# Bidirectional RWKV-7 scan in one kernel: state and v in one contraction, v transposed plainly and centred at the readout

## The chip, the cores and the metric

One core of one Trainium2 chip runs the whole layer in one launch. The metric is the device time in microseconds; less is better. Engines are called as the profile calls them: PE (matmuls, with PEld for its weight loads), DVE (vector), ACT (scalar), POOL and SP (which issues the DMAs).

## The reference, cut to what matters

A layer with two branches that share one input: a bidirectional RWKV-7 time mixing and a gated convolution. The sequence is 256 context and 2048 latent tokens, the width 1024, in 16 heads of 64. The change concerns the scan and its readout:

```python
def step(s, inp):                                  # s: heads x 64 x 64, for each direction
    rt, wt, kt, vt, at, bt = inp
    sa = jnp.einsum('bhij,bhj->bhi', s, at)
    s_new = s * wt[:, :, None, :] + sa[..., None] * bt[:, :, None, :] + vt[..., None] * kt[:, :, None, :]
    y = jnp.einsum('bhij,bhj->bhi', s_new if inclusive else s, rt)
    return s_new, y
...
mu = jnp.mean(y_sum, axis=-1, keepdims=True)       # the readout, per head of 64
var = jnp.mean(jnp.square(y_sum - mu), axis=-1, keepdims=True)
yn = ((y_sum - mu) * lax.rsqrt(var + LNX_EPS)).reshape(b, t, WIDTH_A) * lnx_w + lnx_b
```

## The kernel before, in words

**The first part** (to about 1650 us) projects the input, shifts and mixes it, and writes for each of 8 pairs of heads the factors of the scan to DRAM: `bkD` (b and k), `arD` (a and r), `vD` (v) and `TA`, `TB` (the inverse of the triangular system within a chunk), in fp32.

**The scan** goes over the pairs and, in each, over 36 chunks of 64 tokens; both directions `d` run side by side. Four chunks make a step `g`, of which there are 72. A generator, `prep(g + 1)`, makes the next step ready while `chunk` works on step `g`. Two heads share the 128 partitions, in halves of 64.

`prep` (L801) loads `bk` (one buffer, one DMA), `ar` (two halves, one a head, into a tile with zeros elsewhere, two buffers), `vvz` (one DMA) and six pieces of `Tt`. For each direction it transposes `bk` into `BK` (L828, copied by ACT in L831); multiplies v with `cen`, the matrix that takes the mean over 64 off, which transposes v as well (L835), of which ACT copies the lower half into `UV` (L838); multiplies `bk` with `ar` into the scores (L843), and masks them on DVE into `sc` (L847).

`chunk` (L882) has a chain that goes from one chunk to the next. x is the product of `ar` with the state `Sc` (L887) plus that of the scores `sc` with `UV` (L888), for each direction. Its two diagonal blocks of 64 are copied to `xs`, one by DVE (L890), one by ACT (L891). The product of `Tt` and `xs` (L895) gives u, which ACT puts into the upper half of `UV` (L896). POOL scales the old state (L902), the product of `BK` and `UV` (L909) gives its increment, and one DVE instruction a direction on 128x128 (L910) writes the new state. Beside the chain stand the outputs y (L917, L918), collected by ACT (L931) or DVE (L933).

`readout` (L853) comes twice a pair, for two segments of 512 tokens each time: a square on ACT (L857), a product that sums it over a head (L859), logarithm and exponential on ACT (L860, L863), then scale, gate and store.

**What sets the order.** `tick` (L1243) is called nine times a chunk. It hands out a share of the filling work: the dense fp16 matmuls of the gates and of the convolution's input (L360, with weights split on ACT and DVE in L200 and L201), the 31 taps of the convolution on DVE (L946), and later the projections of the convolution branch (L1106); and every third time a piece of `prep`. The instruction streams of each engine are then ordered by a scheduler when the kernel is built, so what stands behind what on an engine is read from the built order; each engine works off its stream in order.

**After the scan** (from about 3810 us) come the last projections and the output rows.

## Time and profile before

| | |
|---|---|
| three runs | 4125.75, 4129.82, 4140.15 us; median 4129.82 |
| the profiled execution | 4134.31 us, of which the profile's span is 4132.6 us |
| granted TensorE clock, mean | 0.978 of full |
| busy share of the span | PE 93%, PEld 58%, DVE 71%, ACT 47%, POOL 12% |
| chain that ended last, by engine | PE 49%, DVE 29%, ACT 10%, DMA 7%, issue 5% |
| DMA | 528.73 MB, mean 128 GB/s; 298116 of 520450 packets under 512 B |

One execution is profiled. The page first gives shares of the whole span, which mix stages with different limits; then 40 slices of it; then the chain of work that ended last and the costliest groups of instructions by line. A group's row has the count, the busy time, the mean duration, and the idle time of the engine just before its instructions with what ended most of it. Durations of matmuls overlap, so their rate is read from starts in the timeline.

### The profile page before, as it was taken

The numbers are of one execution on the slowest core, as the hardware profiler recorded it, in microseconds if no ns is written. First come the engines' busy times: TensorE is split into PE (matmuls) and PEld (weight loads), VectorE is DVE, ScalarE is ACT, GpSimd is POOL, SyncE is SP. The second block draws the span as 40 slices with busy tenths as digits, with TensorE's granted clock in tenths as the row PEclk, the third lists the DMA queues.
The fourth block names the chain that finished last, engine by engine and source line by source line (L and its number), as shares of the span: only waits on it lengthen the run. The fifth ranks groups of instructions, "written<-read, shape, count | busy, mean of one in ns | idle before, by whom it ended". The sixth has DMA issues, their size and how long they took to land.

```text
span 4132.6 us, 79379 instructions
## 1 busy us (share of the span) xinstructions
PE 3862.6 (93%) x30672; PEld 2396.1 (58%) x30672; DVE 2941.0 (71%) x6826; ACT 1941.7 (47%) x3594; POOL 490.1 (12%) x931
## 2 busy tenths in 40 slices
PE   8999999999999997999999999999999899899999
PEld 3444444444444443777776777777676566786444
DVE  5578788688788777698897998994445774334644
ACT  5666665666666554233324343333444452334522
POOL 0000000000000000231321222221111011110000
PEclk9999999999999998999999999999999999999999
DMA  5344443444444333435334244344535543534632
GB/s 204 126 166 144 158 162 133 138 151 166 141 166 140 139 137 110 92 77 136 70 81 131 71 112 98 85 123 129 142 96 162 161 139 107 156 75 113 203 101 76
DMA packets 520450, 528.73 MB, mean 128 GB/s; under 512 B 298116, under 2 KB 363012, under 8 KB 519560
## 3 DMA queue, kind: packets, MB, share of 16 engines
q1 hardware_dynamic: 520072, 523.66, 42.0%
q8 instruction: 241, 3.95, 0.4%
q14 instruction: 137, 1.12, 0.1%
HBM read 298.01 MB, written 196.35 MB: 120 GB/s over the span
## 4 chain that ended last, share of the span: by engine, by line
PE 49%; DVE 29%; ACT 10%; DMA 7%; issue 5%; SPq 1%; POOL 0%; DVEq 0%; ACTq 0%
PE pg L360 10%; PE pp L1106 5%; DVE acc L946 5%; DVE X L476 3%; DVE tmp L475 3%; PE psc L843 3%; PE px L895 3%; PE psy L909 3%; PE pvt L835 2%; PE px L887 2%; PE py L918 2%; PE py L917 2%; PE px L888 2%; DVE sc L847 1%; DMA wf<-in_w_in_dram 1%
## 5 line engine op out<-in xcount | busy, mean ns | idle before, releaser
L946 DVE SCALAR_TENSOR_TENSOR acc<-z,cw,acc 128x512 f32<-128x512 f32 x960 | 687.3, 750 | 10.9 <-ACT acc L944 3.7
L360 PE MATMUL pg<-hH,whi 128*128 128x512 f16 x1536 | 589.1, 384 | 7.8 <-ACT whi L200 7.0
L360 PE MATMUL pg<-hH,wlo 128*128 128x512 f16 x1536 | 587.5, 383 | 1.8 <-DVE wlo L201 1.8
L360 PE MATMUL pg<-hL,whi 128*128 128x512 f16 x1536 | 588.6, 383 | 0.0
L902 POOL TENSOR_SCALAR pre<-Sc,PL 128x128 f32<-128x128 f32 x560 | 357.6, 648 | 1577.2 <-DVE Sc L910 1438.1
L360 PEld LDWEIGHTS <-whi 128*128 128x128 f16 x3072 | 298.9, 99 | 261.0 <-issue 35.1
L891 ACT ACTIVATE xs<-px 64x128 f32<-64x128 f32 x288 | 78.3, 272 | 552.2 <-DVE xs L890 537.7
L209 PE MATMUL pg<-hH,whi 128*128 128x512 f16 x832 | 318.8, 384 | 4.2 <-ACT hH L279 4.0
L210 PE MATMUL pg<-hL,whi 128*128 128x512 f16 x832 | 319.6, 384 | 0.1
L211 PE MATMUL pg<-hH,wlo 128*128 128x512 f16 x832 | 319.3, 384 | 0.0
L910 DVE SCALAR_TENSOR_TENSOR Sc<-psy,PL,pre 128x128 f32<-128x128 f32 x560 | 173.0, 344 | 195.3 <-PE psy L909 191.5
L847 DVE TENSOR_TENSOR sc<-psc,msk 128x512 f32<-128x512 f32 (+1 forms) x288 | 180.1, 654 | 98.5 <-PE psc L843 97.5
L887 PE MATMUL px<-Sc,arz 128*128 128x128 f32 x1152 | 235.5, 286 | 7.1 <-DVE Sc L910 3.6
L895 PE MATMUL px<-xs,Tt 128*128 128x128 f32 x1152 | 193.8, 291 | 49.1 <-ACT xs L891 46.2
L360 PEld LDWEIGHTS <-wlo 128*128 128x128 f16 x1536 | 152.2, 99 | 134.3 <-issue 17.3
L888 PE MATMUL px<-UV,sc 128*128 128x128 f32 x1152 | 224.2, 276 | 0.0
L895 PEld LDWEIGHTS px<-xs,Tt 128*128 128x128 f32 x1152 | 155.2, 191 | 114.3 <-ACT xs L891 100.8
L843 PE MATMUL psc<-arz,bk 64*128 64x128 f32 (+1 forms) x2304 | 216.4, 290 | 4.7 <-ACT BK L831 2.2
L909 PE MATMUL psy<-UV,BK 128*128 128x128 f32 x1120 | 191.6, 294 | 24.7 <-ACT UV L896 24.6
L843 PEld LDWEIGHTS psc<-arz,bk 64*128 64x128 f32 x2304 | 176.0, 189 | 62.7 <-issue 39.5
L917 PE MATMUL py<-arz,Sc 128*128 128x128 f32 x1024 | 201.2, 278 | 1.8 <-DVE y L933 1.1
L887 PEld LDWEIGHTS px<-Sc,arz 128*128 128x128 f32 x1152 | 180.9, 192 | 34.7 <-DVE Sc L910 11.5
(361 smaller groups left out, 8137.2 us busy)
## 6 DMA issues: line engine op xcount, KB each, us to landing
wf<-in_w_in_dram SPq DMA_DIRECT2D x74, 512.0 KB, 3.7
bk<-bkD SPq DMA_DIRECT2D x72, 512.0 KB, 3.8
arz<-arD SPq DMA_DIRECT2D x144, 256.0 KB, 4.8
bkD<-bk SPq DMA_DIRECT2D x64, 512.0 KB, 2.7
arD<-ar SPq DMA_DIRECT2D x64, 512.0 KB, 3.6
vvz<-vD SPq DMA_DIRECT2D x72, 256.0 KB, 3.2
lt<-loD SPq DMA_DIRECT2D x32, 512.0 KB, 4.8
sh<-raw SPq DMA_DIRECT2D x64, 191.6 KB, 2.4
```

What stands on the lines that cost most here:

```text
L209: PE.matmul(ps, whi[:, k, :], xhi(k), start=(k == 0), stop=False)
L210: PE.matmul(ps, whi[:, k, :], xlo(k), start=False, stop=False)
L211: PE.matmul(ps, wlo[:, k, :], xhi(k), start=False, stop=(k == NK - 1))
L360: PE.matmul(ps, wt[a][:, k, :], b[:, k, o:o + 512], start=(m == 0), stop=(m == 23))
L843: PE.matmul(ps[h][:, c, :nq], bk[h * 64:h * 64 + 64, d, c, :], ar[h * 64:h * 64 + 64, d, c, :nq // 64, h, :], start=True, stop=True)
L887: PE.matmul(px[:, d, :], ar[:, d, c, 0].rearrange("p h l -> p (h l)"), Sc[d][k % 2], start=True, stop=True)
L888: PE.matmul(px[:, d, :], sc[:, d, c, 0].rearrange("p h l -> p (h l)"), UV[:, d, c, :], start=False, stop=True, skip_group_check=True)
L895: PE.matmul(px[:, 2 + d, :], t[:, d, c, :], xs[:, d, :], start=True, stop=True)
L902: G.tensor_scalar(pr, Sc[d][k % 2], pl, 1.0, op0=ALU.mult, op1=ALU.mult)
L909: PE.matmul(psy, BK[:, d, c, :], UV[:, d, c, :], start=True, stop=True)
L917: PE.matmul(o, Sc[d][k % 2], ar[:, d, c, 1].rearrange("p h l -> p (h l)"), start=True, stop=True)
L946: V.scalar_tensor_tensor(acc, z[:, k + 512 * i:k + 512 * i + 512], cw[:, k:k + 1], acc, op0=ALU.mult, op1=ALU.add)
```

## The change

The state gets a tile of its own kind, `SV`, of 128x128 for each chunk and direction: on the diagonal the two states, off the diagonal v of the two heads. The masked scores of the first kind go from `sc` into the zero blocks of `ar`. So x is one product of 128 rows of contraction where there were two, and its blocks off the diagonal are left as they come. `Tt` becomes block diagonal, u is written on the diagonal of `UV` and v off it, `bk` has b and k in swapped order for the second head, and only diagonal blocks of the state's increment are used, so the state update becomes four pieces of 64x64. v is transposed with `ident`, not multiplied with `cen`; the mean is taken off y in the readout, by a product with `cen`. x is copied by one ACT instruction.

```diff
@@ prep
-        nc.sync.dma_start(bk, bkD[p][:, :, ks].rearrange("p d c i l -> p d c (i l)"))
-        ar, vv = ars[g % NAR], vvs[0]
+        nc.sync.dma_start(bk[0:64], bkD[p][0:64, :, ks].rearrange("p d c i l -> p d c (i l)"))
+        for i in range(2):
+            nc.sync.dma_start(bk[64:128, :, :, 64 * i:64 * i + 64], bkD[p][64:128, :, ks, 1 - i, :])
+        ar, SV, vv = ars[g % NAR], SVs[g % NAR], vvz
         for h, hs in enumerate(H2):
             nc.sync.dma_start(ar[hs, :, :, :, h, :], arD[p][hs, :, ks])
-        nc.sync.dma_start(vv[:, :, 64:], vD[p][:, :, 256 * s:256 * s + 256])
+            nc.sync.dma_start(vv[hs, :, 64 * (1 - h):64 * (1 - h) + 256], vD[p][hs, :, 256 * s:256 * s + 256])
...
-        G.memset(UV[0:64], 0.0)
...
-                PE.matmul(pv[:, c, :], vv[:, d, c * 64:c * 64 + P], cen, start=True, stop=True)
...
-            S.activation(UV[64:128, d], pv[64:128], AF.Copy)
+                PE.transpose(pv[:, c, :], vv[:, d, c * 64:c * 64 + P], ident)
+            for x in (SV, UV):
+                for h, hs in enumerate(H2):
+                    S.activation(x[H2[1 - h], d, :, hs], pv[H2[1 - h], :, hs], AF.Copy)
...
             for h in range(2):
-                V.tensor_tensor(sc[:, d, :, :ni, h, :], ps[h].rearrange("p c (i l) -> p c i l", l=64)[:, :, :ni], msk[:, d:d + 1, :nq].rearrange("p o (i l) -> p o i l", l=64).broadcast_to([P, 4, ni, 64]), op=ALU.mult)
+                ho = H2[1 - h]
+                V.tensor_tensor(ar[ho, d, :, 0, h, :], ps[h][ho, :, 0, :], msk[ho, d:d + 1, 0:64].broadcast_to([64, 4, 64]), op=ALU.mult)
+                if s > 0:
+                    V.tensor_tensor(sc[:, d, :, h, :], ps[h][:, :, 1, :], msk[:, d:d + 1, 64:128].broadcast_to([P, 4, 64]), op=ALU.mult)
@@ readout
         for i in ii:
+            pc = pC.tile([P, 512], F32, name="pc", tag="pC")
+            PE.matmul(pc, cen, ys[i], start=True, stop=True)
+            S.activation(ys[i], pc, AF.Copy)
@@ chunk
         for d in range(2):
-            PE.matmul(px[:, d, :], ar[:, d, c, 0].rearrange("p h l -> p (h l)"), Sc[d][k % 2], start=True, stop=True)
-            PE.matmul(px[:, d, :], sc[:, d, c, 0].rearrange("p h l -> p (h l)"), UV[:, d, c, :], start=False, stop=True, skip_group_check=True)
-        xs = xss[k % 2]
-        V.tensor_copy(xs[0:64, :, 0:64], px[0:64, 0:2, 0:64])
-        S.activation(xs[64:128, :, 64:128], px[64:128, 0:2, 64:128], AF.Copy)
+            PE.matmul(px[:, d, :], ar[:, d, c, 0].rearrange("p h l -> p (h l)"), SV[:, d, c, :], start=True, stop=True)
+        xs = bp.tile([P, 2, P], F32, name="xs")
+        S.activation(xs, px[:, 0:2, :], AF.Copy)
...
-        S.activation(UV[0:64, :, c, :], px[0:64, 2:4, :], AF.Copy)
+        for hs in H2:
+            S.activation(UV[hs, :, c, hs], px[hs, 2:4, hs], AF.Copy)
...
-                V.scalar_tensor_tensor(Sc[d][(k + 1) % 2], psy, PL[:, p, d, k + 1:k + 2], pre[d], op0=ALU.mult, op1=ALU.add)
+                for hs in H2:
+                    V.scalar_tensor_tensor(Sn[hs, d, (c + 1) % 4, hs], psy[hs, hs], PL[hs, p, d, k + 1:k + 2], pre[d][hs, hs], op0=ALU.mult, op1=ALU.add)
```

The scheduler orders the new streams anew. Three places in them follow. On PE, the piece of one chunk (the 153rd) from x on, before; `pg` is a dense matmul, its weight loads stand as rows of their own, and a v product and that for u follow:

```order
L887 MATMUL px<-Sc_18661,arz_18648 128x128
L888 MATMUL px<-UV,sc 128x128
L887 MATMUL px<-Sc_18663,arz_18648 128x128
L888 MATMUL px<-UV,sc 128x128
L360 LDWEIGHTS whi
L360 MATMUL pg<-hH,whi 128x512
L360 LDWEIGHTS whi
L360 MATMUL pg<-hL,whi 128x512
L360 LDWEIGHTS wlo
L360 MATMUL pg<-hH,wlo 128x512
L360 LDWEIGHTS whi
L360 MATMUL pg<-hH,whi 128x512
```

and such a piece of the changed kernel, from x to u (its lines have other numbers):

```order
L890 MATMUL px<-SV_18650,arz_18648 128x128 x2
L359 LDWEIGHTS whi
L359 MATMUL pg<-hH,whi 128x512
L359 LDWEIGHTS whi
L359 MATMUL pg<-hL,whi 128x512
L359 LDWEIGHTS wlo
L359 MATMUL pg<-hH,wlo 128x512
L359 LDWEIGHTS whi
L359 MATMUL pg<-hH,whi 128x512
L896 MATMUL px<-xs,Tt_18646 128x128 x2
```

Four products for x have become two; dense matmuls stand between x and u in both. On DVE, a piece of the scan with the convolution before (`acc` is a tap of the convolution):

```order
L847 TENSOR_TENSOR sc<-psc,msk 128x8x64 x2
L890 COPY xs_18652<-px 64x2x64
L946 SCALAR_TENSOR_TENSOR acc<-z,cw,acc 128x512 x3
L910 SCALAR_TENSOR_TENSOR Sc_18660<-psy,PL,pre 128x128
L910 SCALAR_TENSOR_TENSOR Sc_18662<-psy,PL,pre 128x128
L946 SCALAR_TENSOR_TENSOR acc<-z,cw,acc 128x512 x2
L890 COPY xs_18651<-px 64x2x64
```

and of the changed kernel:

```order
L950 SCALAR_TENSOR_TENSOR acc<-z,cw,acc 128x512 x3
L845 TENSOR_TENSOR arz_18649<-psc,msk 64x4x64
L847 TENSOR_TENSOR sc<-psc,msk 128x4x64
L845 TENSOR_TENSOR arz_18649<-psc,msk 64x4x64
L847 TENSOR_TENSOR sc<-psc,msk 128x4x64
L950 SCALAR_TENSOR_TENSOR acc<-z,cw,acc 128x512 x3
L914 SCALAR_TENSOR_TENSOR SV_18651<-psy,PL,pre 64x64 x4
```

The copy of x has left the stream; scores and state come in twice as many pieces, of half and a quarter of the size. On ACT, a readout before, from the copy of x to that of u (`f` and `whi` belong to the filling work):

```order
L891 ACTIVATE xs_18651<-px 64x2x64
L674 ACTIVATE f_23518<-pg,un 128x512
L860 ACT_TABLE_LOAD
L860 ACTIVATE sqy<-pv,eps 128x512 x2
L863 ACT_TABLE_LOAD
L863 ACTIVATE sqy<-sqy 128x512 x2
L200 ACTIVATE whi<-wf,p2s 128x1024
L874 ACTIVATE y<-y,par 128x512 x2
L896 ACTIVATE UV<-px 64x2x128
```

and one of the changed kernel:

```order
L858 ACTIVATE y<-pc 128x512
L860 ACTIVATE sqy<-y 128x512
L898 ACTIVATE UV<-px 64x2x64 x2
L863 ACT_TABLE_LOAD
L863 ACTIVATE sqy<-pv,eps 128x512
L858 ACTIVATE y<-pc 128x512
L866 ACT_TABLE_LOAD
L866 ACTIVATE sqy<-sqy 128x512
L860 ACTIVATE sqy<-y 128x512
L199 ACTIVATE whi<-wf,p2s 128x1024
L877 ACTIVATE y<-y,par 128x512
L863 ACT_TABLE_LOAD
```

The logarithms of the two segments no longer stand side by side, so a readout has four table loads where it had two. Over the whole order the loads at these two lines go from 18 and 18 to 32 and 31, and one more comes at a gate.

## Rows read from the trace of the kernel before

**Rows 1.** Busy tenths of PE and DVE in 40 slices of the span:

```profile
PE   8999999999999997999999999999999899899999
DVE  5578788688788777698897998994445774334644
```

**Rows 2.** Windows of the scan: busy us (count) of PE, PEld, DVE, ACT, POOL:

```profile
1669.00:1819.00 150.00, 145.17 (x1081) 116.33 (x1080) 118.28 (x239) 48.20 (x119) 41.25 (x54) 1.00 0.37 86
1819.00:2783.00 964.00, 925.63 (x6583) 695.22 (x6581) 877.11 (x1796) 353.15 (x726) 237.78 (x301) 1.00 0.39 99
2783.00:3137.00 354.00, 338.08 (x2423) 257.15 (x2422) 170.07 (x454) 144.55 (x297) 53.93 (x108) 1.00 0.47 124
3137.00:3509.00 372.00, 350.62 (x2204) 235.06 (x2203) 223.86 (x497) 159.60 (x327) 42.35 (x77) 0.98 0.50 143
3509.00:3807.00 298.00, 266.47 (x1886) 222.90 (x1885) 115.60 (x304) 103.95 (x230) 46.20 (x103) 0.96 0.46 118
```

**Rows 3.** The same for L887 alone (PE, PEld), four PE records a chunk:

```profile
1819.00:2783.00 964.00, 107.86 (x528) 83.12 (x528) 1.00 0.39 99
2783.00:3137.00 354.00, 38.69 (x192) 30.13 (x193) 1.00 0.47 124
3509.00:3807.00 298.00, 39.71 (x192) 30.54 (x192) 0.96 0.46 118
```

**Rows 4.** Timeline of PE in one chunk (start us, us, what):

```profile
2313.45 0.39 PE L888 MATMUL px<-UV,sc 128*128 128x128 f32 x2
2313.67 0.39 PE L887 MATMUL px<-Sc,arz 128*128 128x128 f32 x2
2313.89 0.39 PE L888 MATMUL px<-UV,sc 128*128 128x128 f32 x2
```

**Rows 5.** Groups on PE (count | busy us, mean ns | idle before, releasers):

```profile
L888 PE MATMUL px<-UV,sc 128*128 128x128 f32 x1152 | 224.2, 276 | 0.0
L835 PE MATMUL pvt<-cen,vvz 128*128 128x128 f32 x1152 | 161.2, 280 | 6.6 <-ACT sqy L860 6.6
L828 PE MATMUL pbk<-ident,bk 128*128 128x128 f32 x576 | 111.4, 279 | 5.3 <-DMA bk<-bkD 2.4 <-DVE sc L847 1.4 <-ACT sqy L860 1.0
```

**Rows 6.** Timeline of DVE in the convolution stretch:

```profile
2310.91 0.59 DVE L910 SCALAR_TENSOR_TENSOR Sc<-psy,PL,pre 128x128 f32<-128x128 f32 x2
2311.43 2.72 DVE L946 SCALAR_TENSOR_TENSOR acc<-z,cw,acc 128x512 f32<-128x512 f32 x4
2314.08 1.27 DVE L847 TENSOR_TENSOR sc<-psc,msk 128x512 f32<-128x512 f32 x2
2315.28 0.27 DVE L890 COPY xs<-px 64x128 f32<-64x128 f32 x1
2315.48 0.73 DVE L946 SCALAR_TENSOR_TENSOR acc<-z,cw,acc 128x512 f32<-128x512 f32 x1
```

**Rows 7.** Groups on DVE, the scores and a product of half their size:

```profile
L847 DVE TENSOR_TENSOR sc<-psc,msk 128x512 f32<-128x512 f32 x256 | 167.6, 683 | 91.1 <-PE psc L843 90.6
L583 DVE TENSOR_TENSOR Asb<-pA,mk 128x256 f32<-128x256 f32 x64 | 26.9, 420 | 48.3 <-PE pA L582 29.9 <-PE pf L497 12.5 <-DMA cu<-Asb 3.4
```

**Rows 8.** Groups on ACT, the copies of v, u and x:

```profile
L838 ACT ACTIVATE UV<-pvt 64x512 f32<-64x512 f32 x144 | 85.1, 591 | 99.2 <-PE pvt L835 98.1
L896 ACT ACTIVATE UV<-px 64x256 f32<-64x256 f32 x288 | 108.1, 375 | 154.0 <-PE px L895 151.2
L891 ACT ACTIVATE xs<-px 64x128 f32<-64x128 f32 x288 | 78.3, 272 | 552.2 <-DVE xs L890 537.7 <-DVE p2t L170 4.7 <-DVE p2s L174 3.3
```

**Rows 9.** Timeline of ACT at a readout, from the copy of x to that of u:

```profile
2900.55 0.27 ACT L891 ACTIVATE xs<-px 64x128 f32<-64x128 f32 x1
2900.84 1.28 ACT L860 ACT_TABLE_LOAD   x1
2902.14 1.26 ACT L860 ACTIVATE sqy<-pv,eps 128x512 f32<-128x512 f32 x2
...
2905.77 0.36 ACT L896 ACTIVATE UV<-px 64x256 f32<-64x256 f32 x1
```

**Rows 10.** DMA issues of the page's last part (count, KB each, us to landing):

```profile
bk<-bkD SPq DMA_DIRECT2D x72, 512.0 KB, 3.8
arz<-arD SPq DMA_DIRECT2D x144, 256.0 KB, 4.8
```

More of the change, by code (lines that the diff above doesn't have):

```diff
@@ L59 @@
 PB = (1,)
-PV = ()
 SWP = 1
@@ L789 @@
     ars = [b1.tile([P, 2, 4, 2, 2, 64], F32, name=f"arz{i}") for i in range(NAR)]
-    vvs = [b1.tile([P, 2, 64 + 256], F32, name=f"vvz{i}") for i in range(1)]
-    xss = [b1.tile([P, 2, P], F32, name=f"xs{i}") for i in range(2)]
-    for t in Tt + ars + xss:
+    SVs = [b1.tile([P, 2, 4, P], F32, name=f"SV{i}") for i in range(NAR)]
+    vvz = b1.tile([P, 2, 64 + 256], F32, name="vvz")
+    for t in Tt + ars:
         G.memset(t, 0.0)
-    for t in vvs:
-        G.memset(t[:, :, 0:64], 0.0)
-    Sc = [[b1.tile([P, P], F32, name=f"Sc{d}{i}") for i in range(2)] for d in range(2)]
+    G.memset(vvz[0:64, :, 0:64], 0.0)
+    G.memset(vvz[64:128, :, 256:320], 0.0)
     st = {}
@@ L816, in prep @@
             o = 64 * h
-            nc.sync.dma_start(t[o:o + 32, :, :, 0:32], ta5[0, :, h, :, ks, :])
-            nc.sync.dma_start(t[o + 32:o + 64, :, :, 32:64], ta5[1, :, h, :, ks, :])
-            nc.sync.dma_start(t[o:o + 32, :, :, 32:64], tb5[:, h, :, ks, :])
-        sc = bp.tile([P, 2, 4, 2, 2, 64], F32, name="sc")
+            nc.sync.dma_start(t[o:o + 32, :, :, o:o + 32], ta5[0, :, h, :, ks, :])
+            nc.sync.dma_start(t[o + 32:o + 64, :, :, o + 32:o + 64], ta5[1, :, h, :, ks, :])
+            nc.sync.dma_start(t[o:o + 32, :, :, o + 32:o + 64], tb5[:, h, :, ks, :])
+        sc = bp.tile([P, 2, 4, 2, 64], F32, name="sc")
         BK = bp.tile([P, 2, 4, P], F32, name="BK")
         UV = bp.tile([P, 2, 4, P], F32, name="UV")
-        G.memset(UV[0:64], 0.0)
         yield
@@ L834, in prep @@
             for c in range(4):
-                PE.matmul(pv[:, c, :], vv[:, d, c * 64:c * 64 + P], cen, start=True, stop=True)
-                if c in PV:
-                    yield
-            S.activation(UV[64:128, d], pv[64:128], AF.Copy)
+                PE.transpose(pv[:, c, :], vv[:, d, c * 64:c * 64 + P], ident)
+            for x in (SV, UV):
+                for h, hs in enumerate(H2):
+                    S.activation(x[H2[1 - h], d, :, hs], pv[H2[1 - h], :, hs], AF.Copy)
             yield
-            ps = [pC.tile([P, 4, P], F32, name="psc", tag="pC") for _ in range(2)]
+            ps = [pC.tile([P, 4, 2, 64], F32, name="psc", tag="pC") for _ in range(2)]
+            ni = 1 if s == 0 else 2
             for c in range(4):
-                for h in range(2):
-                    PE.matmul(ps[h][:, c, :nq], bk[h * 64:h * 64 + 64, d, c, :], ar[h * 64:h * 64 + 64, d, c, :nq // 64, h, :], start=True, stop=True)
-                if c in PY:
-                    yield
+                for h, hs in enumerate(H2):
+                    PE.matmul(ps[h][:, c, :ni, :], bk[hs, d, c, :], ar[hs, d, c, :ni, h, :], start=True, stop=True)
             for h in range(2):
-                V.tensor_tensor(sc[:, d, :, :ni, h, :], ps[h].rearrange("p c (i l) -> p c i l", l=64)[:, :, :ni], msk[:, d:d + 1, :nq].rearrange("p o (i l) -> p o i l", l=64).broadcast_to([P, 4, ni, 64]), op=ALU.mult)
+                ho = H2[1 - h]
+                V.tensor_tensor(ar[ho, d, :, 0, h, :], ps[h][ho, :, 0, :], msk[ho, d:d + 1, 0:64].broadcast_to([64, 4, 64]), op=ALU.mult)
+                if s > 0:
+                    V.tensor_tensor(sc[:, d, :, h, :], ps[h][:, :, 1, :], msk[:, d:d + 1, 64:128].broadcast_to([P, 4, 64]), op=ALU.mult)
             yield
-        st[g] = dict(ar=ar, sc=sc, BK=BK, UV=UV)
+        st[g] = dict(ar=ar, sc=sc, BK=BK, UV=UV, SV=SV)
     ys = {}
@@ L901, in chunk @@
                 pl = PL[:, p, d, k + 1:k + 2]
-                G.tensor_scalar(pr, Sc[d][k % 2], pl, 1.0, op0=ALU.mult, op1=ALU.mult)
+                G.tensor_scalar(pr, SV[:, d, c, :], pl, 1.0, op0=ALU.mult, op1=ALU.mult)
                 pre.append(pr)
@@ L906, in chunk @@
         if k < NCH - 1:
+            Sn = SVs[(p * 9 + (k + 1) // 4) % NAR]
             for d in range(2):
@@ L916, in chunk @@
                 o = py[:, d, c % 2, :]
-                PE.matmul(o, Sc[d][k % 2], ar[:, d, c, 1].rearrange("p h l -> p (h l)"), start=True, stop=True)
-                PE.matmul(o, UV[:, d, c, :], sc[:, d, c, 1].rearrange("p h l -> p (h l)"), start=False, stop=True, skip_group_check=True)
+                PE.matmul(o, SV[:, d, c, :], ar[:, d, c, 1].rearrange("p h l -> p (h l)"), start=True, stop=True)
+                PE.matmul(o, UV[:, d, c, :], sc[:, d, c].rearrange("p h l -> p (h l)"), start=False, stop=True, skip_group_check=True)
                 if d == 0:
@@ L1262 @@
         if s == 0:
-            for d in range(2):
-                V.memset(Sc[d][0], 0.0)
+            for hs in H2:
+                V.memset(SVs[g % NAR][hs, :, 0, hs], 0.0)
         prv[0] = prep(g + 1) if g + 1 < NSTEP else None
```

4 lines of the change are left out of this document (1 added, 3 removed).

## The prediction

> **What bounds the kernel now.** I read the slices first, because they show where the scan begins: from the seventeenth slice on, PE stays at nine tenths, while DVE is near full only as long as the convolution runs, and then falls to four tenths [rows 1]. So I cut the scan into five stretches and asked for the busy time of each engine [rows 2]. They are: a start; the long stretch with the convolution (DVE busy 877 of 964 us); a stretch where the dense matmuls L360 still run but the convolution is over (DVE 170 of 354); one in which the projections of the convolution branch ride along; and a last one with nearly no filling work. The matmuls of L887 come four records to a chunk, so their counts give the pace [rows 3]: 528 records are 132 chunks at 964 / 132 = 7.30 us, 192 are 48 chunks at 354 / 48 = 7.38 us, and the last 48 chunks take 298 / 48 = 6.21 us. The reader is to see this: with the convolution and without it a chunk takes the same time, so DVE, although it is 91% busy in the first, does not set the pace. PE does, being 95 to 96% busy in both. In the last stretch PE falls to 89%, and the chain inside a chunk shows.
>
> **What goes from PE.** In a run of matmuls the starts lie 0.22 us apart for one fp32 product of two records [rows 4]: L888 at 2313.45, the next at 2313.67, the next at 2313.89. That is 0.11 us a record; the longer durations overlap. The change drops L888: 1152 records by 0.11 = 127 us [rows 5]. The v products of L835 have 1152 records for 576 products, whereas the transposes of L828 have 576 records for as many results [rows 5]; v is now a transpose, so 576 records go, 63 us. The readout adds 32 products of 512 columns, four times as wide as those at 0.22: 0.88 us each, 28 us. Net: 127 + 63 - 28 = **162 us less on PE**, or 162 / 288 = 0.56 us a chunk. The number of scores, of state and of y products is as before.
>
> **What DVE gains and loses.** The copy of x goes: 288 by 0.20 us (2315.28 to the next start at 2315.48 [rows 6]) = 58 us. The state update is cut in four: two pieces of 128x128 took 0.52 us to the next start (2310.91 to 2311.43 [rows 6]), 0.26 each. No row shows a 64x64 piece. From above it costs as much as the whole, 0.26; from below half, 0.13. The convolution steps, four times as long, start 0.66 us apart (2.65 us to 2314.08 for four [rows 6]), a slope of 0.40 us for 384 columns, so 64 columns fewer save 0.07: I take 0.19. Then 1120 by 0.19 less 560 by 0.26 = 213 - 146 = +67 us (bounds 0 and +146). The scores: 256 of 128x512 at 683 ns and 32 of the size of L583 at 420 ns [rows 7] make 188 us; after it 288 + 256 = 544 pieces of 256 columns at 420 ns make 228: +40. Net **+49 us**, 0.17 a chunk (bounds -18 to +128). What DVE also loses is a wait: before, the copy stood among the convolution steps and waited for PE, and ACT's half of x waited for it.
>
> **What ACT gets.** Four copies of 64x256 for one of 64x512: 576 by 375 ns less 144 by 591 = +131 us; x as one 128x256 piece, which I price as 64x256, 375 for 272 ns, 288 times: +30; u in two pieces of 64x128, 272 ns each, for one of 375: 288 by 169 ns = +49 [rows 8]. The readout adds 32 copies of 128x512, about 0.6 us as the 64x512 of L838: +19. The instruction order of the change has 63 table loads at the logarithm and the exponential where there were 36, and one more elsewhere: 28 by 1.28 us [rows 9] = +36. Together **+265 us** on an engine that is 353 / 964 = 37% busy in the convolution stretch [rows 2], so it will stand near half. Most of it runs beside PE's dense matmuls. The readout's part does not: there the copy of u, which the chain needs, stands behind both table loads, 2900.55 to 2905.77 [rows 9]. So I charge the 19 + 36 = 55 us of the readout in full, and of the rest nothing.
>
> The row shows a table load of 1.28 us and the next ACTIVATE 0.02 us after its end (2900.84, 2902.14). The Trainium skill (ScalarE: Activation LUTs, What ACT_TABLE_LOAD costs) adds a drain of 1380 ns to each switch of the set. By that rule, an estimate, 28 loads would take 74 us and the sum would come out 38 us later; the trace shows no such drain behind the load, so I do not use it.
>
> **What is moved or small.** POOL loses 72 memsets of u, which nothing waits for. Per step SP issues bk in three pieces and v in two, three DMAs more; the second half of bk now lands in runs of 256 bytes, as ar does. Bk has one buffer, but its first reader L828 waited for DMA 2.4 us in the whole run [rows 5], so I take nothing.
>
> **The sum, by stretch.** With the convolution, PE alone would allow 7.30 - 0.56 = 6.74 us a chunk, but DVE needs 877 / 132 = 6.64 + 0.17 = 6.81 us busy, and it idled 9% before; at 2 to 4% idle it gives 7.0: 0.3 us by 132 chunks, 40 us. At the start 24 chunks by 0.3: 7 us. The two middle stretches, 48 and 36 chunks, keep PE as their bound: 84 by 0.56 = 47 us. In the last one the chain counts: two products fewer in it, and one ACT piece in place of a DVE copy and an ACT copy one behind the other, against longer u and state steps: I take 0.5 us by 48 = 24 us. That is 118 us saved, less 55 us at the readouts: **63 us**. The profiled execution took 4134.3 us (span 4132.6 and 1.7 around it), the median of three runs is 4129.8, 4.5 lower. 4134.3 - 63 - 4.5 = **4067 us**, 1.5% faster.
>
> **The rivals.**
> 1. *PE's whole share comes back.* If the table loads hide under the dense matmuls, and DVE, rid of the wait for x, packs the convolution without idle time, the pace is PE's everywhere: 4130 - 162 = 3968 us. For it: the equal pace with and without the convolution [rows 3]. Against it: DVE at 91% [rows 2].
> 2. *DVE becomes the bound.* With 0.26 us for a quarter of the state update DVE needs 6.64 + 128 / 288 = 7.08 us a chunk, and at the old 9% of idle time no chunk of the first two stretches is faster: 47 us of the gain go, and 71 - 55 = 16 us remain: 4114 us, the edge of what can be told; a little more on the state pieces and nothing changes. For it: 877 of 964 us. Against: two of its waiting points per chunk become one.
> 3. *ACT takes the chain* (slower). If x and u have to queue behind the v copies in ACT's order, as they do behind the readout [rows 9], the extra 265 us lie on the path and PE's 162 us do not help: +103 us, 4233 us. It decides from where 162 / 265 = 61% of the added ACT time is exposed. Against it: ACT is 37% busy and each of the two ACT hops of a chunk has over 3 us of PE work in its pace to hide a copy of 0.4 us.
> 4. *The short runs delay bk* (slower). Before, bk's 512 KB landed in 3.8 us, ar's 256 KB, in runs of 256 bytes, in 4.8 [rows 10]. By ar's rate the second half of bk takes 4.8 us in place of 1.9, 2.9 us a step, 72 by 2.9 = 209 us if PE waits for all of it: 4067 + 209 = 4276 us. It decides from where the slack between the last score product of a step and the first transpose of the next is under that. Against it: 2.4 us of wait in all. The Trainium skill (DMA: Bandwidth & Descriptors, Specifications) asks for 512 B or more for the full rate; the two rows agree that the shorter runs are slower per byte.
>
> That the change does not do what it says is no rival: its instruction order holds 576 products for x and 576 transposes of v.
>
> **How the numbers follow.** The forecast, from about 4020 to 4105, gets 0.52; rival 1, 0.20; rival 2, 0.13; rival 3, 0.10; rival 4, 0.05. A measurement of this kernel can tell about 0.3%, 12 us, from no change. The forecast and rival 1 are faster by more; of rival 2 half is; a slower end needs rival 3 or 4, or rival 2 with dear pieces: 0.76 faster, 0.09 the same, 0.15 slower. The range leaves out most of rivals 3 and 4 and a little below rival 1: 3960 to 4160 us.
>
> **What would show it.** Right: L888 gone, L835's successor with 576 records, chunks of about 7.0 us with the convolution and 6.8 without, DVE at 95% or more in the convolution stretch, ACT near half, more ACT time between x and u at the readouts. Wrong: a chunk without the convolution that still takes 7.3 us (then PE was not the bound but the chain), a 64x64 state piece of 0.26 us or over, transposes of bk that wait for DMA, or x waiting long behind v copies on ACT.

## The result: slower by 1%, and the profile after

Five runs of the changed kernel have a median of 4175.36 us (4161.45 to 4180.63), five of the kernel before, beside them on the same chip, 4136.47. The ratio is 1.0100, 95% interval 1.0084 to 1.0116: some 40 us slower. 4067 was forecast, and 4175 lies above the range. The profiled execution has a span of 4171.0 us against 4132.6, 38.4 more, which the traces divide below.

The first part of the page of the changed kernel (busy us, share, instructions):

```profile
PE 3834.4 (92%) x29008; PEld 2294.2 (55%) x29008; DVE 3081.4 (74%) x7354; ACT 2191.0 (53%) x4374; POOL 362.2 (9%) x858
```

The page before had 3862.6 us and 30672 records on PE, 2941.0 us on DVE, 1941.7 us on ACT. The 1664 records are gone from PE as counted. ACT has 249 us more (265 were worked out), DVE 140 more (49 were).

The slices of the changed kernel, beside [rows 1]:

```profile
PE   7999999999999997999999999999999898888999
DVE  5577787788788687899989999999566773334644
PEclk9999999999999998999999999999999998799999
```

PE, which stood at nine tenths to the last slices of the scan, is at eight there, and the granted clock falls to seven tenths. So I cut the scan by chunks, at the same chunks in both kernels: at the 24th, 168th, 204th and 240th of 288. These are the windows of the changed kernel from the 24th chunk on, columns as in [rows 2]:

```profile
1810.60:2869.70 1059.10, 983.89 (x6366) 698.00 (x6365) 978.06 (x2154) 512.21 (x1191) 159.14 (x290) 0.98 0.43 99
2869.70:3125.20 255.50, 245.15 (x1599) 175.13 (x1599) 163.33 (x429) 143.73 (x321) 37.49 (x70) 1.00 0.55 136
3125.20:3494.50 369.30, 343.19 (x1997) 222.85 (x1996) 241.88 (x564) 190.67 (x425) 32.99 (x70) 0.95 0.55 144
3494.50:3832.50 338.00, 278.71 (x1575) 222.56 (x1576) 130.94 (x384) 140.51 (x349) 37.21 (x92) 0.85 0.44 103
```

and the first and last of the same stretches before:

```profile
1819.30:2871.30 1052.00, 1009.98 (x7198) 760.50 (x7197) 924.01 (x1920) 386.91 (x799) 252.48 (x329) 1.00 0.40 102
...
3509.20:3799.60 290.40, 258.87 (x1840) 217.90 (x1840) 113.25 (x298) 103.31 (x228) 46.09 (x103) 0.96 0.47 119
```

From the starts of x in each chunk:

| stretch (chunks) | before, us | after, us | change | forecast, before the 55 us for readouts |
|---|---|---|---|---|
| start (0 to 23) | 150.3 | 136.3 | -14.0 | -7 |
| convolution (24 to 167) | 1052.0 | 1059.1 | +7.1 | -40 |
| dense matmuls alone, then projections (168 to 239) | 637.9 | 624.8 | -13.1 | -47 |
| nearly no filling work (240 to 286) | 290.5 | 338.0 | +47.5 | -24 |
| ahead of the scan and behind it | | | +10.8 | 0 |

Together they are the 38.4 us, but for rounding. The forecast had cut its stretches at chunk 156 in place of 168, so 12 chunks of its -47 stand in the second row here. Of the last row's 10.8, 5.3 us lie ahead of the scan, where the two programs do the same; the first x starts anywhere from 1666.8 to 1677.9 us in the executions profiled here. Neither the convolution stretch nor the last does what was forecast, and the last alone loses more than the whole. The price is visible where one chunk hands over to the next. The following times are means over the chunks of a stretch (of the last stretch its first 36, chunks 240 to 275), worked out from the starts and ends of their instructions (us; "to" is the time from the end of one to the start of the next; for u it begins at the start of its product, for the state at the start of psy):

| | x product | to copy | copy of x | to u product | to copy of u | copy of u | to psy | to state | state | to next x | sum |
|---|---|---|---|---|---|---|---|---|---|---|---|
| convolution, before | 1.16 | 1.03 | 0.27 | 0.35 | 1.04 | 0.38 | 0.59 | 1.03 | 0.68 | 0.84 | 7.37 |
| convolution, after | 0.90 | 0.35 | 0.38 | 0.44 | 1.22 | 0.57 | 0.54 | 1.46 | 1.33 | 0.25 | 7.43 |
| last, before | 1.40 | 0.72 | 0.27 | 0.23 | 0.91 | 0.38 | 0.13 | 0.63 | 0.70 | 0.47 | 5.85 |
| last, after | 1.64 | 0.28 | 0.38 | 0.20 | 0.92 | 0.61 | 0.30 | 0.72 | 1.49 | 0.37 | 6.91 |

With the convolution the front of the chain wins what was meant (0.26 at the products of x, 0.68 at the wait for its copy). The back loses it: the state takes 0.65 longer and begins 0.43 later, and that the next x follows it sooner (0.25 in place of 0.84) only makes it even.

The groups of the changed kernel that answer to [rows 5, 7, 8]:

```profile
L914 DVE SCALAR_TENSOR_TENSOR SV<-psy,PL,pre 64x64 f32<-64x64 f32 x1120 | 316.1, 282 | 195.8 <-PE psy L912 175.3
L890 PE MATMUL px<-SV,arz 128*128 128x128 f32 x1152 | 231.6, 305 | 38.1 <-DVE SV L914 33.1 <-DVE arz L845 1.0
L898 ACT ACTIVATE UV<-px 64x128 f32<-64x128 f32 x576 | 154.9, 269 | 143.3 <-PE px L896 139.6
L845 DVE TENSOR_TENSOR arz<-psc,msk 64x256 f32<-64x256 f32 x288 | 120.6, 419 | 126.4 <-PE psc L842 122.1
L892 ACT ACTIVATE xs<-px 128x256 f32<-128x256 f32 x288 | 110.0, 382 | 422.1 <-PE px L890 420.4
L836 ACT ACTIVATE UV<-pvt 64x256 f32<-64x256 f32 x288 | 108.9, 378 | 5.2
L836 ACT ACTIVATE SV<-pvt 64x256 f32<-64x256 f32 x288 | 108.9, 378 | 66.9 <-PE pvt L833 63.1
L826 PE MATMUL pbk<-ident,bk 128*128 128x128 f32 x576 | 108.2, 285 | 3.9 <-DVE sc L847 2.6 <-DVE p2t L169 0.9
L847 DVE TENSOR_TENSOR sc<-psc,msk 128x256 f32<-128x256 f32 x256 | 106.3, 415 | 2.1
L833 PE MATMUL pvt<-ident,vvz 128*128 128x128 f32 x576 | 93.4, 282 | 10.1 <-ACT sqy L863 9.2 <-ACT BK L829 0.7 <-DVE p2s L173 0.2
L863 ACT ACT_TABLE_LOAD x32 | 41.1, 1283 | 0.6
L866 ACT ACT_TABLE_LOAD x31 | 39.8, 1283 | 0.5
```

The prices taken for ACT (375, 272) and for the scores (420) are met within 7 ns, and the 63 table loads are there; in front of the copy of x ACT idles 422 us, 420 of them for PE. The state pieces are the exception, as the timeline of DVE shows (start us, us, what):

```profile
2317.32 2.33 DVE L950 SCALAR_TENSOR_TENSOR acc<-z,cw,acc 128x512 f32<-128x512 f32 x3
2319.68 1.20 DVE L914 SCALAR_TENSOR_TENSOR SV<-psy,PL,pre 64x64 f32<-64x64 f32 x4
2320.91 4.69 DVE L950 SCALAR_TENSOR_TENSOR acc<-z,cw,acc 128x512 f32<-128x512 f32 x6
```

From 2319.68 to 2320.91 four pieces take 1.23 us of DVE's stream, 0.31 each, where a piece of four times the size took 0.26 [rows 6]. By that, 1120 pieces cost 347 us where 560 cost 146: +201, not +67, and above the upper bound of +146.

Where other instructions stand between the pieces, the trace shows which of them are dear:

```profile
2342.36 0.27 DVE L914 SCALAR_TENSOR_TENSOR SV<-psy,PL,pre 64x64 f32<-64x64 f32 x1
2342.55 0.13 DVE L168 TENSOR_SCALAR p2t<-p2t 128x1 int32<-128x1 int32 x1
2342.72 0.29 DVE L914 SCALAR_TENSOR_TENSOR SV<-psy,PL,pre 64x64 f32<-64x64 f32 x1
2343.04 0.15 DVE L169 TENSOR_SCALAR p2t<-p2t 128x1 int32<-128x1 int32 x1
```

The first piece of a pair works on partitions 0 to 63, and an instruction on all 128 starts 0.19 us after it, before it has ended. The second works on partitions 64 to 127, and the like instruction starts only after 0.32 us, when it has ended. Over the whole trace, where DVE did not idle between the two, the next start comes 0.20 us (median) after a lower piece if an instruction on all partitions follows (50 cases), 0.29 if the upper piece follows (496), and 0.32 after an upper piece, whatever follows (476 of 479). So the dear part is the step from one half of the partitions to the other and back, at which the pieces do not overlap; two whole pieces of 128x128 do, 344 ns long and 0.26 us apart.

The last stretch is read in the timeline. On ACT after, in a chunk in which the next step's v arrives:

```profile
3563.91 0.39 ACT L892 ACTIVATE xs<-px 128x256 f32<-128x256 f32 x1 [2.48 <-PE px L890]
3564.28 0.60 ACT L829 ACTIVATE BK<-pbk 128x512 f32<-128x512 f32 x1
3564.89 0.77 ACT L836 ACTIVATE SV<-pvt 64x256 f32<-64x256 f32 x2
3565.68 0.77 ACT L836 ACTIVATE UV<-pvt 64x256 f32<-64x256 f32 x2
3566.36 0.54 ACT L898 ACTIVATE UV<-px 64x128 f32<-64x128 f32 x2
```

and before, in the like place:

```profile
3510.93 0.27 ACT L891 ACTIVATE xs<-px 64x128 f32<-64x128 f32 x1 [4.29 <-DVE xs L890]
3511.27 0.60 ACT L831 ACTIVATE BK<-pbk 128x512 f32<-128x512 f32 x1
3512.06 0.38 ACT L896 ACTIVATE UV<-px 64x256 f32<-64x256 f32 x1 [0.19 <-PE px L895]
3512.73 0.59 ACT L838 ACTIVATE UV<-pvt 64x512 f32<-64x512 f32 x1 [0.29 <-PE pvt L835]
```

Before, the copy of v stood behind that of u; after, four copies, 1.5 us, stand ahead of it. On PE (after) this is what follows:

```profile
3564.52 0.61 PE L896 MATMUL px<-xs,Tt 128*128 128x128 f32 x4
3566.95 0.71 PE L912 MATMUL psy<-UV,BK 128*128 128x128 f32 x4 [1.82 <-ACT UV L898]
3569.71 1.06 PE L890 MATMUL px<-SV,arz 128*128 128x128 f32 x4
3571.30 1.22 PE L896 MATMUL px<-xs,Tt 128*128 128x128 f32 x4 [0.53 <-ACT xs L892]
```

PE idles 1.82 us for u, and two chunks' like products show the second effect: four records at L896 take 0.61 us and, 7 us later, 1.22. The granted clock has gone from one of its levels to the other, 2.4 to 1.2 GHz. Windows of 10 us of the changed kernel, a little earlier:

```profile
3510.00:3520.00 10.00, 7.24 (x37) 6.33 (x36) 3.03 (x10) 2.38 (x7) 0.74 (x2) 0.72 0.34 52
3520.00:3530.00 10.00, 9.47 (x25) 5.92 (x25) 1.60 (x4) 4.06 (x8) 0.01 (x1) 0.50 0.52 109
```

PE was idle for 2.8 of 10 us, and in the next window the clock is 0.50 throughout. So the table's last two rows mix a longer chain with a slower PE.

### The profile page after: what moved, and what is told of

Same layout as the page of the kernel before. It is cut to its first block, busy times and chain, and to the rows that moved or that the text cites. A ratio compares the mean times of both kernels' runs of the same rounds, so it can differ in the third digit from the quotient of the medians.

```text
span 4171.0 us, 78507 instructions
## 1 busy us (share of the span) xinstructions
PE 3834.4 (92%) x29008; PEld 2294.2 (55%) x29008; DVE 3081.4 (74%) x7354; ACT 2191.0 (53%) x4374; POOL 362.2 (9%) x858
## 5 line engine op out<-in xcount | busy, mean ns | idle before, releaser
L914 DVE SCALAR_TENSOR_TENSOR SV<-psy,PL,pre 64x64 f32<-64x64 f32 x1120 | 316.1, 282 | 195.8 <-PE psy L912 175.3
L904 POOL TENSOR_SCALAR pre<-SV,PL 128x128 f32<-128x128 f32 x560 | 295.1, 527 | 1852.5 <-DVE SV L914 1715.6
L892 ACT ACTIVATE xs<-px 128x256 f32<-128x256 f32 x288 | 110.0, 382 | 422.1 <-PE px L890 420.4
L842 PE MATMUL psc<-arz,bk 64*128 64x128 f32 (+1 forms) x2304 | 278.4, 298 | 12.0 <-ACT UV L836 7.9
L842 PEld LDWEIGHTS psc<-arz,bk 64*128 64x128 f32 x2304 | 228.7, 197 | 84.2 <-issue 48.5
L890 PE MATMUL px<-SV,arz 128*128 128x128 f32 x1152 | 231.6, 305 | 38.1 <-DVE SV L914 33.1
L898 ACT ACTIVATE UV<-px 64x128 f32<-64x128 f32 x576 | 154.9, 269 | 143.3 <-PE px L896 139.6
L890 PEld LDWEIGHTS px<-SV,arz 128*128 128x128 f32 x1152 | 174.0, 196 | 101.9 <-DVE SV L914 39.7
L896 PE MATMUL px<-xs,Tt 128*128 128x128 f32 x1152 | 194.3, 292 | 37.9 <-ACT xs L892 37.6
L845 DVE TENSOR_TENSOR arz<-psc,msk 64x256 f32<-64x256 f32 x288 | 120.6, 419 | 126.4 <-PE psc L842 122.1
L896 PEld LDWEIGHTS px<-xs,Tt 128*128 128x128 f32 x1152 | 164.2, 197 | 84.5 <-ACT xs L892 71.6
L921 PE MATMUL py<-arz,SV 128*128 128x128 f32 x1024 | 206.4, 284 | 3.5 <-ACT y L935 1.8
```

What stands on the lines that cost most here:

```text
L842: PE.matmul(ps[h][:, c, :ni, :], bk[hs, d, c, :], ar[hs, d, c, :ni, h, :], start=True, stop=True)
L890: PE.matmul(px[:, d, :], ar[:, d, c, 0].rearrange("p h l -> p (h l)"), SV[:, d, c, :], start=True, stop=True)
L896: PE.matmul(px[:, 2 + d, :], t[:, d, c, :], xs[:, d, :], start=True, stop=True)
L904: G.tensor_scalar(pr, SV[:, d, c, :], pl, 1.0, op0=ALU.mult, op1=ALU.mult)
L914: V.scalar_tensor_tensor(Sn[hs, d, (c + 1) % 4, hs], psy[hs, hs], PL[hs, p, d, k + 1:k + 2], pre[d][hs, hs], op0=ALU.mult, op1=ALU.add)
L921: PE.matmul(o, SV[:, d, c, :], ar[:, d, c, 1].rearrange("p h l -> p (h l)"), start=True, stop=True)
```

## The experiments

Verdicts are ratios to the kernel before, run beside each on the same chip; 0.01 is 41 us, and differences between two variants are taken from their ratios. The changed kernel stands at 1.0100. Each variant is scheduled anew, so an experiment changes the order of the streams along with the work that it adds or leaves out.

### The state in four pieces, in the kernel before

```diff
-                V.scalar_tensor_tensor(Sc[d][(k + 1) % 2], psy, PL[:, p, d, k + 1:k + 2], pre[d], op0=ALU.mult, op1=ALU.add)
+                for hs in H2:
+                    V.scalar_tensor_tensor(Sc[d][(k + 1) % 2][hs, hs], psy[hs, hs], PL[hs, p, d, k + 1:k + 2], pre[d][hs, hs], op0=ALU.mult, op1=ALU.add)
```

> The kernel before, with its state update alone cut into four pieces of 64x64 (the blocks off the diagonal are never used). Theory D (state pieces): a piece of 64x64 costs DVE as much as one of 128x128, about 0.30 us, and the two pieces more stand in the chain of every chunk, so this alone makes the kernel before slower by 0.3 to 0.6 us a chunk where the chain sets the pace: 40 to 120 us, 4175 to 4255 us. Theory A (ACT: the copies of v and u and the readout): no change, 4125 to 4150 us.

Measured: 4214.29 us, ratio 1.0194 (1.0173 to 1.0215): 80 us for the pieces alone, inside theory D's range. With the convolution the state step went from 0.68 to 1.36 us a chunk and the chunk from 7.37 to 7.72. The piece costs what it costs in the changed kernel:

```profile
L913 DVE SCALAR_TENSOR_TENSOR Sc<-psy,PL,pre 64x64 f32<-64x64 f32 x1120 | 316.5, 283 | 197.3 <-PE psy L911 174.3 <-POOL pre L904 0.5
```

### The state in one piece, in the changed kernel

```diff
-                for hs in H2:
-                    V.scalar_tensor_tensor(Sn[hs, d, (c + 1) % 4, hs], psy[hs, hs], PL[hs, p, d, k + 1:k + 2], pre[d][hs, hs], op0=ALU.mult, op1=ALU.add)
+                V.scalar_tensor_tensor(Sn[:, d, (c + 1) % 4, :], psy, zc, pre[d], op0=ALU.mult, op1=ALU.add)
```

> The changed kernel with the state update written as one 128x128 instruction a direction again. It overwrites v, and the increment is multiplied by zero in the same instruction, so that numbers stay finite: the state's increment and the contribution of v to x are left out. The number of instructions on PE, ACT and POOL stays as in the changed kernel. Theory 1 (the four state pieces lie in the chain of a chunk and cost a fixed price each): the step from the first piece to the last falls from 1.33 to about 0.7 us, and the whole by 60 to 85 us, as the pieces cost the kernel before 83 us: 4090 to 4115 us, with the last 47 chunks back near 300 us. Theory 2 (the pieces are hidden in the stretches with filling work, and what is lost is lost to ACT and the clock): less than 25 us, above 4150 us.

Measured: 4119.39 us, ratio 0.9970 (0.9954 to 0.9986), 54 us less than the changed kernel, 4 us above what theory 1 gave and far below theory 2. The state step with the convolution is 0.63 us, and the stretch is 36 us shorter than the changed kernel's 1059.1. But the last 47 chunks take 331.6 us, not about 300: that half of theory 1 falls. Windows, the convolution and the last stretch:

```profile
1808.70:2831.70 1023.00, 962.20 (x6365) 689.77 (x6364) 932.40 (x1936) 512.53 (x1191) 246.15 (x292) 0.98 0.43 104
3445.60:3777.20 331.60, 269.92 (x1578) 218.23 (x1577) 107.88 (x291) 140.55 (x349) 35.52 (x92) 0.87 0.44 104
```

DVE was cut from 131 to 108 us in the last stretch, and 6 us came of it; the clock stays at 0.87. The pieces cost most where DVE is full: 36 us with the convolution, where it is 92% busy in the changed kernel, 16 with the projections, and nothing with the dense matmuls alone, where the chunks took 5 us longer without them.

### v centred in the step's preparation, nothing in the readout

```diff
-                PE.transpose(pv[:, c, :], vv[:, d, c * 64:c * 64 + P], ident)
+                PE.matmul(pv[:, c, :], vv[:, d, c * 64:c * 64 + P], cen, start=True, stop=True)
...
-            pc = pC.tile([P, 512], F32, name="pc", tag="pC")
-            PE.matmul(pc, cen, ys[i], start=True, stop=True)
-            S.activation(ys[i], pc, AF.Copy)
```

> The changed kernel, with v centred in the preparation again (a product with the centring matrix instead of a transpose) and no centring at the readout. PE has 35 us more work, ACT 55 us less. Theory A: the readouts hold up the chain by 3 to 5 us at each of 16 places, so 40 to 70 us come back, 4105 to 4135 us. Theory D: the readouts count little, 4160 to 4190 us.

Measured: 4137.71 us, ratio 1.0005 (0.9993 to 1.0017), 39 us less than the changed kernel, although PE has 63 - 28 = 35 us more to do; that is 3 us above theory A's range and far below theory D's. So the plain transposes and the centring of y together lose: what PE saves is worth less than 32 more copies and 28 more table loads on ACT. The last 47 chunks take 324.4 us in place of 338.0.

### The second copy of v on POOL

```diff
-            for x in (SV, UV):
-                for h, hs in enumerate(H2):
-                    S.activation(x[H2[1 - h], d, :, hs], pv[H2[1 - h], :, hs], AF.Copy)
+            for h, hs in enumerate(H2):
+                S.activation(SV[H2[1 - h], d, :, hs], pv[H2[1 - h], :, hs], AF.Copy)
+            for h, hs in enumerate(H2):
+                G.tensor_copy(UV[H2[1 - h], d, :, hs], SV[H2[1 - h], d, :, hs])
```

> The changed kernel, with the second copy of v (the one into UV) made by POOL out of the first, so that ACT does two copies of v per step and direction instead of four, some 110 us less in all. Theory A: u waits less behind copies of v, 30 to 80 us come back, 4095 to 4145 us. Theory D: nothing, 4160 to 4190 us.

Measured: 4150.92 us, ratio 1.0048 (1.0032 to 1.0064), 21 us less than the changed kernel, between the two theories: something came back, less than theory A asked for. The last 47 chunks take 322.7 us in place of 338.0; with the convolution, 1062.7 in place of 1059.1, nothing came.

### Both repairs

> Both partial repairs at once: v centred where it is transposed, nothing in the readout, and the second v copy made by POOL. Alone they gained 38 and 25 us. Theory 1 (two separate costs on ACT, at the readouts and at the steps): they add up, 4105 to 4120 us, faster than the kernel before by about 0.4%. Theory 2 (both buy the same relief): 4130 to 4140 us, no difference to the kernel before.

Measured: 4124.81 us, ratio 0.9985 (0.9976 to 0.9995): 47 us less than the changed kernel, of the 60 that the two gave apart. That lies between the theories; the two gains seem to overlap in part. It is below the kernel before by 0.15%, less than executions of one kernel differ among themselves; as a version it is a draw. The stretch with the convolution (1050.0 us) has not become shorter than before:

```profile
1810.70:2860.70 1050.00, 970.23 (x6622) 704.71 (x6620) 995.31 (x2166) 429.32 (x1014) 251.70 (x434) 0.99 0.42 100
```

DVE is busy for 995 of 1050 us there, 95%: with less on ACT, DVE looks like the bound, and the next experiment, which takes work from DVE, shortens the stretch to 1015.3.

### Both repairs and the state in one piece

> The two repairs and the whole state update of one 128x128 instruction (with the same parts left out: the state's increment and v's contribution to x). Theory 1 (state pieces, v copies and readout are what ate the freed PE time): 4020 to 4050 us, the prediction's figure or below, that is 80 us or more under the kernel before; chunks without the convolution near 6.8 us. Theory 2 (something else holds the chain, such as the two copies of u): above 4075 us.

Measured: 4065.70 us, ratio 0.9847 (0.9827 to 0.9867): 104 us less than the changed kernel, and 54 + 47 = 101 were measured apart. So the pieces on the one side and ACT's work on the other add up, as separate costs do; 4065.7 is also above the 4050 of theory 1, and below the 4075 of theory 2. v being centred in the preparation, 127 us of PE are saved here, 0.44 a chunk. By stretches against the kernel before: start -12.5, convolution -36.7, dense matmuls alone 265.9 to 248.6 (-17.3), projections -24.3, last +16.7. In the stretch that PE bounds, 36 chunks give 17.3 us, and 36 x 0.44 is 16: there all of PE's share has come. PE's filling work in each stretch is the same in both kernels. The projections gave 24.3 for the same share of 16, which PE's work alone does not explain. With the convolution 36.7 of 63 have come, and the table's terms show where the rest is: from the start of x to the copy of u a chunk takes 3.00 us where it took 3.85 before, but the state begins 1.65 us after the start of psy in place of 1.03, and the copies of u take 0.56 in place of 0.38.

### The convolution on DVE left out

29 of DVE's 30 taps a block gone, in each of the two kernels (of the 31 taps the first is ACT's):

```diff
-                V.scalar_tensor_tensor(acc, z[:, k + 512 * i:k + 512 * i + 512], cw[:, k:k + 1], acc, op0=ALU.mult, op1=ALU.add)
+                if k < 2:
+                    V.scalar_tensor_tensor(acc, z[:, k + 512 * i:k + 512 * i + 512], cw[:, k:k + 1], acc, op0=ALU.mult, op1=ALU.add)
```

> The kernel before, with 29 of the 30 taps of the convolution on DVE left out (its output is not the layer's; the order and pace of all else stay). Before, a chunk took 7.31 us with the taps and 7.39 without them, so DVE did not set the pace: theory P (PE and the chain set it) expects 7.1 to 7.4 us a chunk in the stretch that held the taps, a change of under 30 us. If DVE did set the pace there, the chunk falls to under 7.0 us and 50 us or more go.

> The changed kernel with the same 29 taps left out. Theory D' (in the stretch with the convolution DVE, with its many small pieces, has become the bound and eats what PE gave up): the chunk falls from 7.35 to 6.7 to 7.0 us over 144 chunks, 50 to 90 us, and this kernel is then faster than the kernel before with the same taps left out. If the longer chain through ACT holds that stretch instead, it stays at 7.2 us or more and the two kernels without taps are alike.

Measured: 4110.93 us, ratio 0.9951 (0.9929 to 0.9972), for the kernel before, and 4116.47, 0.9969 (0.9950 to 0.9989), for the changed one. Without the taps the first gains 20 us, the second 54: DVE's crowding costs the changed kernel almost three times as much. Its own window of that stretch:

```profile
1809.20:2814.10 1004.90, 961.54 (x6366) 694.78 (x6366) 458.65 (x1387) 511.23 (x1191) 110.00 (x291) 0.97 0.45 107
```

There a chunk of the changed kernel takes 6.98 us, at the edge of what theory D' gave, but the whole kernel is not faster than the kernel before without taps: the stretch has 1004.9 us against 1030.0 there, 25 us of PE's 81 (144 x 0.56), and the last 47 chunks lose it again, 329.8 against 287.6. The taps explain the late state: without them it begins 0.81 us after the start of psy in place of 1.46, in the kernel before 0.84 in place of 1.03. DVE's load is not all, though. At 46% busy the longer back of the chain (state 1.26 us, copies of u 0.58) still takes most of PE's share.

### Unread matmuls where there is no filling work

```diff
         while "ready" not in c_:
+            if npad % 3 == 0:
+                pd = pG.tile([P, 512], F32, name="pd", tag="pG")
+                PE.matmul(pd, wa[0][:, 0, 0, :], wa[0][:, 0, 0:4, :].rearrange("p k e -> p (k e)"), start=True, stop=True)
+            npad += 1
             yield
```

> The changed kernel with one dense matmul whose result nobody reads added to every third call of the waiting branch, some 360 in all, in the stretch of the scan that has no filling work. Theory C (there PE now idles enough for its clock to be at 1.2 GHz half of the time, mean granted clock 0.76 and 0.77 where it was 0.89 and 0.97, and the chain is made of fp32 products at that rate): the clock is at 0.97 or more in that stretch, its 47 chunks take 295 to 315 us instead of 338, and the kernel 4130 to 4155 us instead of 4175. If the stretch is longer because of ACT and the small pieces, the added work does not help or costs: 4170 to 4200 us.

> The kernel before with the same added matmuls. Theory C: its clock was already at 0.89 to 1.00 there, so there is little to win: 4115 to 4145 us. If added work helps for another reason than the clock, it helps this one by as much as the changed kernel.

Measured: 4153.35 us, ratio 1.0069 (1.0045 to 1.0092), for the changed kernel with them, and 4159.79, 1.0071 (1.0049 to 1.0092), for the kernel before with them. Work that nobody reads costs the kernel before 29 us and seems to give the changed one 13; the kernel before was to stay within 4115 to 4145 by theory C, and missed that. The intervals of the changed kernel with them and without overlap, so the trace must say it; it is of the fastest of the five executions, 4144.45 us. Last 47 chunks, changed kernel with them:

```profile
3487.10:3804.70 317.60, 302.12 (x1939) 218.06 (x1940) 129.93 (x384) 139.85 (x349) 40.96 (x92) 0.98 0.46 109
```

The clock is 0.98 there in place of 0.85, and the stretch 20 us shorter. The kernel before, whose clock was 0.96 already, got 28 us longer there (290.5 to 318.5). So, an estimate from these two pairs, the clock's part of the 47.5 us is 20 at least, and up to all of it if the matmuls are as much in the way as they are before; more narrowly it was not settled.

With both repairs the same was tried once more:

> The same, and unread dense matmuls in the stretch without filling work, which gained the changed kernel 22 us by keeping the granted clock up. Theory 1 (the clock still falls without them): another 10 to 20 us, 4090 to 4110 us. Theory 2 (the shorter chain leaves PE busy enough that the clock holds, and the added matmuls are in the way, as in the kernel before, where they cost 30 us): 4125 to 4145 us.

Measured: 4127.89 us, ratio 0.9991 (0.9981 to 1.0002). The last stretch takes 314.8 us at a clock of 0.98, and without the added matmuls 315.6 at 0.91: no gain, no loss. The time lies in theory 2's range, but its reason does not hold as it stands: the clock had not held without the added matmuls, and they were not in the way.

### The decay folded into bk, a miss

POOL scales `bk` once a step, so the state becomes an addition for both directions at once, two pieces a chunk of 64x2x64 instead of four (`xs` has one buffer here, not two):

```diff
+            G.tensor_tensor(bks[:, d, :n], bk[:, d, :n], PL[:, p, d, 4 * s + 1:4 * s + 1 + n].unsqueeze(2).broadcast_to([P, n, P]), op=ALU.mult)
...
+            for hs in H2:
+                V.tensor_tensor(Sn[hs, :, (c + 1) % 4, hs], psy[hs, :, hs], pr[hs, :, hs], op=ALU.add)
```

> The changed kernel, with the decay of the increment taken into BK (POOL scales bk before the transpose), so that the state update becomes two additions of 64x2x64 over both directions, where there were four pieces of 64x64 each with a scalar of its own. Theory D: the state update falls from 1.33 to about 0.7 us in the chain of each chunk and DVE loses some 150 us of work; 0.3 to 0.6 us a chunk come back, 60 to 150 us, 4025 to 4115 us. Theory A: nothing on the chain, 4160 to 4190 us.

Measured: 4176.76 us, ratio 1.0107 (1.0090 to 1.0125): nothing gained. The state step with the convolution fell from 1.33 to 0.60 us, but the wait ahead of it rose from 1.46 to 1.82 and the one behind it from 0.25 to 0.84. Groups of this kernel:

```profile
L951 DVE SCALAR_TENSOR_TENSOR acc<-z,cw,acc 128x512 f32<-128x512 f32 x960 | 739.1, 801 | 17.1 <-ACT acc L949 4.2
L906 POOL TENSOR_SCALAR pre<-SV,PL 128x128 f32<-128x128 f32 x560 | 335.4, 610 | 1572.1 <-DVE SV L915 1428.2 <-ACT SV L839 81.0 <-DVE p2t L168 10.8
L826 POOL TENSOR_TENSOR bks<-bk,PL 128x512 f32<-128x512 f32 x144 | 173.7, 1225 | 83.0 <-DMA bk<-bkD 63.5 <-PE pg L359 9.6 <-PE px L893 6.8
```

The taps take 801 ns in place of 753 and 49 us more in all, while POOL is busy for 574 us in place of 362. The 94 taps that ran mostly beside the product `bks` took 1.20 us in the mean, the 564 beside which POOL did nothing 0.74; that is 42 of the 49. One `psy` tile for both directions also makes each wait for the other. Which of the two ate the gain was not separated; the experiment does not speak against the price of the pieces, which the two runs above settle.

## Why the prediction was wrong, point by point

**PE's 162 us.** Right as work: the records that were to go are gone. The reading that PE and not DVE set the pace before held too: without the taps the kernel before gains only 22 us in the convolution stretch. With the state in one piece, v centred in the preparation and one v copy on POOL, the stretch that PE bounds is shorter by about PE's share. Wrong as time in the changed kernel, since the state pieces, the readouts and the v copies ate it.

**The state piece, taken at 0.19, bounds 0.13 to 0.26.** This is the first step that failed. It measured 0.31 from start to start, above the bound: a slope of 0.40 us for 384 columns was carried down to 64 columns and a quarter of the area, and a small piece was taken to cost at most the whole one. The piece takes 282 ns where the whole takes 344, but four of them in a row start 0.29 and 0.32 us apart in turn. The 0.19 taken is what a lower piece measures when an instruction on all partitions follows, 0.20; what the step left out is the change between the halves of the partitions, of which its rows have no example. Price: 54 us in the changed kernel, 80 in the kernel before. The Trainium skill (VectorE: DVE Perf Modes, The TRN2 errata) says that an instruction of VectorE that reads SBUF pays a fixed latency that shows between instructions, so that many small tiles pay it each. The trace agrees as far as a lower piece of a quarter of the size still takes 0.20 us of the stream where the whole takes 0.26; that an upper piece takes 0.32 goes beyond it. The rule speaks against this change, and the prediction did not weigh it. A state piece of 0.26 us or over was its own sign of being wrong.

**"At 2 to 4% idle it gives 7.0."** DVE's 6.8 us a chunk were met (978.06 / 144 = 6.79, with 22 of 824 taps pushed past the stretch), its idle time was not: 8% as against 12% by these windows, at 7.36 us a chunk. Taking away the wait for x did not pack DVE, as the wait for psy in the same chunk stayed and, with the taps in front of the state, grew from 1.03 to 1.46 us. That is rival 2, "at the old 9% of idle time no chunk of the first two stretches is faster", with its dear pieces.

**ACT: 55 us charged for the readouts, nothing for the rest.** The first half is right in kind: without the readout's part, and with 35 us more on PE, the kernel gains 39. The rest was not free: half of the v copies cost 21 us, by the traces 15 of it in the last stretch, where they stand ahead of u in ACT's order. Rival 3 named that place; its price, 103 us, was for all of ACT's added time on the path.

**The last stretch, -24.** This is the largest miss, +47.5: it has no filling work, so a chain that waits there leaves PE idle, and the idle PE lost its clock, 20 us or more of it. The prediction's row of that stretch showed 0.96 [rows 2], and it asked of no row what becomes of the clock when PE has less to do and the same waits.

**Short runs of bk** (rival 4) cost nothing, as taken: the transposes no longer wait for DMA at all (L826 above), and the DMA part of the page after shows

```profile
bk<-bkD SPq DMA_DIRECT2D x72, 256.0 KB, 3.7
bk<-bkD SPq DMA_DIRECT2D x144, 128.0 KB, 3.8
vvz<-vD SPq DMA_DIRECT2D x144, 128.0 KB, 2.9
```

**What the account covers.** Pieces, readouts and v copies make 101 to 104 us. The kernel without them is 64 us faster than before, of the 127 us of PE that it saves; the rest lies in the chain that is left. With the convolution that is above all the state that waits among the taps (1.65 us after the start of psy where 1.03 was), then the two copies of u (0.56 where 0.38 was); in the last stretch, 307.2 us at a clock of 0.92, it is an emptier PE. That part was read from traces and not tried by itself in this kernel.

## What to carry to other kernels

Work taken from the engine that looks full comes back as time only where that engine, and not the chain between the engines, sets the end: price what the saved product makes necessary on the other engines, and at the pieces' own start-to-start time, since here a quarter of a tile on the upper half of the partitions took more of DVE's stream than the whole. Look at the stretch with the least filling work first, because there the chain is bare, and each wait may also cost the matmul clock. A repair is judged by undoing each new cost alone and then all at once, which shows whether they add up.
